# Both MLPs of a two-layer encoder by one level of Strassen's scheme: seven block products for eight

## The chip, the cores and the metric

The kernel runs on one core of one Trainium2 chip. The metric is the time of one execution on the device, in microseconds (us). The kernel before took 2733.05 us (median of three runs, 2729.04 to 2734.89). Every time below is of these runs or of one profiled execution of the same kernel. A core's engines run side by side and wait for one another through semaphores: PE (TensorE: matrix products, with its weight loads as PEld), DVE (VectorE), ACT (ScalarE), POOL (GpSimd) and SP (SyncE, which issues the transfers).

## What is computed

Two layers on a residual stream x of 1024 tokens by 1024 channels, float32. Layer 0 has differential attention beside an S5 state-space mixer, layer 1 a bidirectional HGRN2 recurrence. After each mixer stands an MLP, which is all that matters here:

```python
h = rmsnorm(x, norm_mlp_g[l])
x = x + jnp.square(jax.nn.relu(h @ w_ff_in[l])) @ w_ff_out[l]   # 1024 -> 4096 -> 1024
```

At the end comes one more RMSNorm.

## The kernel before

x stays in SBUF for the whole kernel as eight tiles `xT[d]`, 128 channels by 1024 tokens each. Every float32 product is made of three products of a reduced float format (fp32r): each operand is cut into a high part and the remainder, and wh·xh, wl·xh and wh·xl are summed in PSUM. `split` (L89 to L96) does the cutting: ACT casts the high part (L92, or L95 with a factor), and DVE or POOL subtracts it to get the low part (L93, or L96 with a factor). `load_w` (L98) brings a 512 KB weight tile (`raw`) and splits it. `mm_part` (L107 to L121) issues the matmuls, 512 columns each, with a weight load of its own for each.

An MLP (`mlp`, L192 to L235) takes `xg`, the split tiles of x times the norm's gain, which are made while the product before still runs (`new_xg`, called from the hooks `done`, `fin` and `last`). The factor R of each token, 1/rms, is applied behind the first product. The work goes by eight chunks of 512 hidden channels. Stage 1 of a chunk is four tiles of 48 matmuls: the product into PSUM (`big`), relu times R on DVE (L201), the square on POOL (L203), and a split. Stage 2 is eight tiles of 24 matmuls, each added to `xT[d]` by DVE from PSUM (L230). So the squares never leave SBUF, and each MLP has 3072 matmuls: 1536 in either product. In the last MLP the last chunk runs by token ranges (512, 256, 256), so that the final norm and the stores of one range lie beside the products of the next (L1207 is the final scaling).

The order of the instructions on each engine is fixed when the program is built: a scheduler places them by a simulated timeline (L1299), and each engine then runs its list in order. An instruction whose operand is late holds up everything behind it on its engine. Around the MLPs the code says: mixer 0, `out_even` (the attention's output projection and `new_xg`), `mlp`, mixer 1, `last_mlp`.

## Time and profile before

| | us |
|---|---|
| median of three runs | 2733.05 |
| the profiled execution, first to last instruction | 2730.3 |
| first MLP, about | 607 to 1310 |
| second MLP, about | 2031 to 2725 |
| PE busy over the span | 2627.0 (96%) |
| DVE busy | 1472.9 (54%) |
| ACT busy | 702.0 (26%) |
| POOL busy | 621.5 (23%) |

The profile describes one execution; its span is 2.75 us under the median of the runs, and inside their scatter. Busy shares are averages over stages with different limits: DVE's 54% is made of some 80 to 90% in the S5 part and a third in the MLPs. A timeline row gives the start, the duration and, in brackets, how long the engine had been idle and which engine's instruction ended that. Of two instructions in a row on one engine the second may start a little before the first's end, so the pace of an engine is read from start to start.

### The profile page before, as it was taken

To read this page: it belongs to the slowest core of one execution; us is meant where nothing else is said; L and a number is where in the kernel's file an instruction comes from. 1 tells how busy PE (TensorE), PEld (TensorE's weight loads), DVE (VectorE), ACT (ScalarE), POOL (GpSimd) and SP (SyncE) were. 2 spreads that over 40 slices of the span, in tenths; PEclk is the share of its full clock that TensorE was granted. 3 is DMA by queue.
4 is the path that set the end of the run, shared out by engine and by line. 5 is a ranking of instruction groups with operands and counts; after the bars stand their busy time and mean duration, and the time that the engine had idled before them with its cause. 6 is when DMAs were issued, how large, how long until landed. Compare 5 with 4: busy or idle time off the path is not lost.

```text
span 2730.3 us, 30693 instructions
## 1 busy us (share of the span) xinstructions
PE 2627.0 (96%) x12784; PEld 2201.2 (81%) x12784; DVE 1472.9 (54%) x1827; ACT 702.0 (26%) x1084; POOL 621.5 (23%) x403
## 2 busy tenths in 40 slices
PE   6878889999999999999999999999999999999997
PEld 5766778888888888888888888888888888888886
DVE  8788967665333233333576766666673333333336
ACT  3333356653111111111321222222241111111114
POOL 5555421111011101110122222222221111011102
PEclk9898999999999999999999999999999999999999
DMA  3222272301111111111111111111111111111112
GB/s 144 59 77 78 86 218 63 93 16 48 47 47 47 53 48 47 47 51 51 48 39 39 39 39 39 39 39 39 33 45 47 47 49 52 47 47 47 54 47 70
DMA packets 50554, 154.51 MB, mean 57 GB/s; under 512 B 7024, under 2 KB 13808, under 8 KB 50416
## 3 DMA queue, kind: packets, MB, share of 16 engines
q1 hardware_dynamic: 50416, 152.56, 17.7%
q8 instruction: 101, 1.65, 0.3%
q14 instruction: 37, 0.30, 0.0%
HBM read 131.56 MB, written 14.68 MB: 54 GB/s over the span
## 4 chain that ended last, share of the span: by engine, by line
PE 84%; DVE 10%; DMA 2%; issue 1%; ACT 1%; SPq 1%; POOL 1%; POOLq 0%; DVEq 0%; ACTq 0%
PE big L117 71%; PE sm L686 2%; PE big L1051 1%; PE sm L117 1%; PE sm L1007 1%; PE big L1022 1%; PE big L651 1%; PE big L652 1%; DVE z L514 1%; PE sm L676 1%; DVE z L517 1%; PE big L586 1%; DVE wl L93 1%; DMA raw<-w 1%; DMA kk<-dk 0%
## 5 line engine op out<-in xcount | busy, mean ns | idle before, releaser
L117 PE MATMUL big<-hi,wh 128*128 128x512 f32 x2000 | 627.0, 394 | 9.4 <-ACT hi L95 7.7
L117 PE MATMUL big<-lo,wh 128*128 128x512 f32 x2000 | 624.0, 393 | 10.9 <-DVE lo L96 10.9
L117 PE MATMUL big<-hi,wl 128*128 128x512 f32 x2000 | 623.0, 392 | 0.0
L92 ACT CAST wh<-raw 128x1024 fp32r<-128x1024 f32 x200 | 210.2, 1051 | 1375.0 <-PE big L117 1224.7
L117 PEld LDWEIGHTS big<-lo,wh 128*128 128x128 f32 x2000 | 376.5, 189 | 92.5 <-DVE lo L96 13.8
L117 PEld LDWEIGHTS big<-hi,wh 128*128 128x128 f32 x2000 | 374.9, 189 | 87.2 <-ACT hi L95 7.7
L117 PEld LDWEIGHTS big<-hi,wl 128*128 128x128 f32 x2000 | 377.3, 189 | 79.3 <-issue 0.2
L203 POOL TENSOR_TENSOR a<-a 128x1024 f32<-128x1024 f32 x64 | 172.8, 2701 | 1111.6 <-DVE a L201 1110.4
L230 DVE TENSOR_TENSOR x<-x,big 128x1024 f32<-128x1024 f32 x120 | 146.3, 1220 | 365.9 <-PE big L117 365.9
L117 PE MATMUL big<-ah,wl 128*128 128x512 f32 (+1 forms) x1008 | 314.6, 390 | 1.2 <-DVE wl L93 1.2
L117 PE MATMUL big<-ah,wh 128*128 128x512 f32 (+1 forms) x1008 | 313.5, 388 | 1.6 <-DVE x L220 1.6
L117 PE MATMUL big<-al,wh 128*128 128x512 f32 (+1 forms) x1008 | 311.5, 387 | 0.0
L201 DVE SCALAR_TENSOR_TENSOR a<-big,R 128x1024 f32<-128x1024 f32 x64 | 78.2, 1224 | 326.3 <-PE big L117 315.7
L117 PEld LDWEIGHTS big<-al,wh 128*128 128x128 f32 x1008 | 189.2, 188 | 41.9
L117 PEld LDWEIGHTS big<-ah,wl 128*128 128x128 f32 x1008 | 189.4, 188 | 41.5 <-DVE wl L93 1.6
L117 PEld LDWEIGHTS big<-ah,wh 128*128 128x128 f32 x1008 | 189.4, 188 | 41.1 <-DVE x L220 2.5
L93 POOL TENSOR_TENSOR wl<-raw,wh 128x1024 fp32r<-128x1024 f32 x58 | 139.4, 2403 | 333.5 <-ACT wh L92 325.0
L93 DVE TENSOR_TENSOR wl<-raw,wh 128x1024 fp32r<-128x1024 f32 x142 | 176.2, 1241 | 14.6 <-ACT wh L92 14.6
L93 DVE TENSOR_TENSOR al<-a,ah 128x1024 fp32r<-128x1024 f32 x64 | 80.7, 1260 | 169.2 <-ACT ah L92 169.1
L92 ACT CAST ah<-a 128x1024 fp32r<-128x1024 f32 x64 | 67.1, 1049 | 187.9 <-POOL a L203 187.9
L653 DVE TENSOR_REDUCE low<-big 128x1 f32<-128x1024 f32 x64 | 77.3, 1220 | 19.4 <-PE big L652 19.1
L655 ACT ACTIVATE E<-big,low 128x1024 f32<-128x1024 f32 x64 | 71.9, 1124 | 30.0 <-DVE low L653 30.0
(345 smaller groups left out, 3021.3 us busy)
## 6 DMA issues: line engine op xcount, KB each, us to landing
raw<-w SPq DMA_DIRECT2D x202, 512.0 KB, 3.3
x<-x SPq DMA_DIRECT2D x16, 512.0 KB, 8.2
sw<-qraw SPq DMA_DIRECT2D x32, 128.0 KB, 2.3
qa<-dq SPq DMA_DIRECT2D x16, 256.0 KB, 6.0
qb<-dq SPq DMA_DIRECT2D x16, 256.0 KB, 7.0
kk<-dk SPq DMA_DIRECT2D x16, 256.0 KB, 7.6
toep<-KK SPq DMA_DIRECT2D x64, 32.0 KB, 2.0
dq<-qh SPq DMA_DIRECT2D x4, 512.0 KB, 2.6
```

Source lines behind the costliest of these rows:

```text
L92: nc.scalar.copy(hi, src)
L93: (eng or nc.vector).tensor_tensor(lo, src, hi, ALU.subtract)
L117: nc.tensor.matmul(ps[:, t], a[:, s], b[:, t], start=(first and i == 0 and j == 0), stop=(last and i == n - 1 and j == 2),)
L201: nc.vector.scalar_tensor_tensor(a, ps, 0.0, R, ALU.max, ALU.mult)
L203: nc.gpsimd.tensor_tensor(sq, a, a, ALU.mult)
L230: nc.vector.tensor_tensor(xT[d], xT[d], ps, ALU.add)
L514: v.tensor_tensor_scan(fl(y, f)[:, 1:], fl(dec, f)[:, 0:last], fl(z, f)[:, 0:last], 0.0, ALU.mult, ALU.add)
L517: v.tensor_tensor_scan(fl(y, r)[:, 0:last][:, ::-1], fl(dec, r)[:, 1:][:, ::-1], fl(z, r)[:, 1:][:, ::-1], 0.0, ALU.mult, ALU.add,)
L586: self.nc.tensor.transpose(ps[:, 128 * j : 128 * j + 128], src[:, col0(j)], self.ident)
L653: v.tensor_reduce(low[:, c : c + 1], S, axis=AX.X, op=ALU.min)
L655: nc.scalar.activation(e, S, AF.Exp, bias=low[:, c : c + 1], scale=-1.0, accum_out=lsum[:, c : c + 1])
L686: nc.tensor.matmul(po, wT[:, k, :], A["V"][:, k, :], start=(k == 0), stop=(k == NT - 1))
```

## The change

Both products of both MLPs go by one level of Strassen's scheme in Winograd's form. The weights are cut in 2 by 2 blocks (`r11` to `r22`), and so are the activations (channels in two halves, tokens in two halves of 512). Seven block products then stand for eight, and each operand of a product is a block or a sum of blocks, formed on the chip in float32 and split afterwards.

- `combos` makes the seven right sides of two 128-channel tiles from four 512-column blocks: four POOL instructions (L253) and seven splits (`h` by ACT, `l` by DVE, L103). `left_sides` does the same for the weights: four loads, four POOL instructions (L316 to L324), seven splits.
- `seven` issues the seven products (in the order 1, 6, 5, 7, 2, 3, 4) into three PSUM banks a, b, c, of which there are two sets. ACT copies product 1 away (L349); DVE forms `v` and `w` from bank b less product 1 (L351, L353), since bank b goes on accumulating. Each product has 12 matmuls in a full step.
- `stage1`: 16 steps of 84 matmuls give 256 hidden channels each. DVE subtracts and applies relu times R, ACT squares, and the squares go to DRAM, 1 MB a step.
- `stage2` reads the squares back (`second_rows`), forms their right sides and adds the products to x: four DVE and three POOL instructions a step (L402 to L411). A step takes 512 hidden channels, half of them new: the right sides lie in four slots, of which the new pair takes two. The first and the last step take one pair alone, with 6 matmuls a product.
- `entry` makes the right sides of the first product from x, behind the mixer's last addition; `tail` does the last 512 hidden channels of the last MLP plainly (192 matmuls), with the final norm by token ranges as before.
- x is loaded earlier (`load_xT` ahead of the attention), and buffers are cut anew. HGRN2's operands are made after the first MLP's end.

An MLP's first product then has 16 × 84 = 1344 matmuls. The second has 14 steps of 84 and 4 of 42 in the first MLP, 1344; in the last MLP 12 of 84, 4 of 42 and the tail's 192, so 1368.

```diff
+    def combos(self, slots, rows):
+        gp = self.nc.gpsimd
+        Ts = [{} for _ in slots]
+        def put(p, srcs):
+            for T, slot, src in zip(Ts, slots, srcs):
+                pool = self.t01 if slot < 2 else self.t23
+                T[p] = tuple(self.half(f"{n}{slot % 2}{p}", pool=pool, dt=F32R) for n in "hl")
+                self.split(*T[p], src)
+        def each(op, outs, lefts, rights):
+            for o, x, y in zip(outs, lefts, rights):
+                gp.tensor_tensor(o, x, y, op)
+        b11, b12, b21, b22 = ([r[:, k] for r in rows] for k in range(4))
+        t2 = [self.half("t2", 2) for _ in slots]
+        put(1, b11)
+        each(ALU.subtract, b11, b11, b12)
+        each(ALU.add, t2, b22, b11)
+        put(6, t2)
+        put(5, b11)
+        each(ALU.subtract, b12, b12, b22)
+        put(7, b12)
+        put(2, b21)
+        put(3, b22)
+        each(ALU.subtract, t2, b21, t2)
+        put(4, t2)
+        return Ts
+    def entry(self, xT, gbase):
+        nc = self.nc
+        Ts = []
+        for i in range(4):
+            y = self.pe.tile([P, 4, 512], F32, tag="ar", name="y", bufs=2)
+            for j in range(2):
+                d = i + 4 * j
+                nc.scalar.activation(
+                    y[:, 2 * j : 2 * j + 2], xT[d].rearrange("p (h t) -> p h t", h=2), AF.Copy, scale=self.gcol(gbase, d)
+                )
+            Ts += self.combos((i if gbase == 16 else (i + 2) % 4,), [y])
+        self.square_sum(xT, PAIRED, "a0", "a1")
+        return Ts
...
+    def left_sides(self, src, n):
+        nc = self.nc
+        gp = nc.gpsimd
+        c = 128 * n
+        r = {}
+        for k, (tag, bufs) in enumerate((("r11", 2), ("r12", 1), ("r21", 2), ("r22", 2))):
+            r[tag] = self.half(tag, bufs, self.pv)[:, 0:c]
+            nc.sync.dma_start(r[tag], src[k])
+        def put(x):
+            hi, lo = (self.half(t, 7, self.pv, F32R)[:, 0:c] for t in ("wh", "wl"))
+            self.split(hi, lo, x)
+            return hi, lo
+        s1, s2 = (self.half(t, 1, self.pv)[:, 0:c] for t in ("s1", "s2"))
+        gp.tensor_tensor(s1, r["r21"], r["r22"], ALU.add)
+        gp.tensor_tensor(s2, s1, r["r11"], ALU.add)
+        yield put(r["r11"])
+        yield put(s2)
+        yield put(s1)
+        gp.tensor_tensor(r["r21"], r["r21"], r["r11"], ALU.add)
+        yield put(r["r21"])
+        yield put(r["r12"])
+        gp.tensor_tensor(s2, s2, r["r12"], ALU.add)
+        yield put(s2)
+        yield put(r["r22"])
+    def seven(self, src, Ts, take):
+        nc = self.nc
+        n = len(Ts)
+        left = self.left_sides(src, n)
+        a, b, c = (self.ps_f.tile([P, 512], F32, tag=t, name=t) for t in "abc")
+        bank = {1: a, 2: a, 6: b, 7: b, 4: b, 5: c, 3: c}
+        p1, vv, ww = self.half("p1"), self.half("v"), self.half("w")
+        v = nc.vector
+        for p in PRODUCTS:
+            hi, lo = next(left)
+            for i in range(n):
+                s = slice(128 * i, 128 * i + 128)
+                th, tl = Ts[i][p]
+                for j, (x, y) in enumerate(((hi, th), (lo, th), (hi, tl))):
+                    nc.tensor.matmul(
+                        bank[p], x[:, s], y,
+                        start=(p in (1, 6, 5) and i == 0 and j == 0), stop=(i == n - 1 and j == 2),
+                        skip_group_check=True,
+                    )
...
+    def stage1(self, l, Ts, spill):
+        nc = self.nc
+        v = nc.vector
+        R = [self.R[:, 0:512], self.R[:, 512:1024]]
+        for j in range(FF // 256):
+            out = self.pe.tile([P, 4, 512], F32, tag="ar", name="sq")
+            def put(k, src):
+                t = self.half("ct", 3)
+                if k != 0:
+                    v.tensor_tensor(t, *src, ALU.subtract)
+                    src = (t,)
+                v.scalar_tensor_tensor(t, src[0], 0.0, R[k % 2], ALU.max, ALU.mult)
+                nc.scalar.activation(out[:, k], t, AF.Square)
+            def take(p, a, b, c, p1, vv, ww):
+                if p == 7:
+                    put(3, (ww, c))
+                elif p == 2:
+                    put(0, (a,))
+                elif p == 3:
+                    put(1, (c, vv))
+                elif p == 4:
+                    put(2, (b, p1))
+            self.seven(self.io[f"win{l}"][j], Ts, take)
+            nc.sync.dma_start(spill[j], out.rearrange("p k t -> p (k t)"))
+    def second_rows(self, k, l, spill):
+        rows = []
+        for j in (2 * k, 2 * k + 1):
+            y = self.pe.tile([P, 4, 512], F32, tag="ar", name="y", bufs=2)
+            self.nc.sync.dma_start(y.rearrange("p k t -> p (k t)"), spill[j])
+            rows.append(y)
+        return self.combos((0, 1) if k % 2 != l else (2, 3), rows)
+    def stage2(self, src, Ts, qs, xT, fin=None):
+        v, gp = self.nc.vector, self.nc.gpsimd
+        for n, q in enumerate(qs):
+            (x11, x12), (x21, x22) = ((xT[d][:, 0:512], xT[d][:, 512:1024]) for d in (q, q + 4))
+            def take(p, a, b, c, p1, vv, ww):
+                if p == 7:
+                    v.tensor_tensor(x22, x22, c, ALU.subtract)
+                    gp.tensor_tensor(x22, x22, ww, ALU.add)
+                elif p == 2:
+                    v.tensor_tensor(x11, x11, a, ALU.add)
+                elif p == 3:
+                    v.tensor_tensor(x12, x12, c, ALU.add)
+                    gp.tensor_tensor(x12, x12, vv, ALU.subtract)
+                elif p == 4:
+                    v.tensor_tensor(x21, x21, b, ALU.add)
+                    gp.tensor_tensor(x21, x21, p1, ALU.subtract)
+            self.seven(src[n], Ts, take)
+            if fin:
+                fin(q)
+    def mlp(self, l, xT, Ts, fin=None):
+        spill = [self.pd.tile([P, 2048], F32, tag=f"sq{j}", name=f"sq{j}") for j in range(FF // 256)]
+        self.open_sums()
+        self.stage1(l, Ts, spill)
+        self.open_sums()
+        four, two = self.io[f"wout{l}"], self.io[f"wtwo{l}"]
+        rows = lambda k: self.second_rows(k, l, spill)
+        now = rows(0)
+        self.stage2(two[0], now, (2, 3), xT)
+        for k in range(1, 8 - l):
+            new = rows(k)
+            self.stage2(four[k - 1], now + new, (0, 1) if k % 2 else (2, 3), xT, fin if k == 7 else None)
+            now = new
+        self.stage2(two[1], now, (2, 3) if l == 0 else (0, 1), xT, fin)
...
+    def tail(self, xT, spill):
+        nc, io = self.nc, self.io
+        v = nc.vector
+        self.close_fast(2)
+        with self.pool("tl") as pt:
+            acts = []
+            for j in (14, 15):
+                y = self.pe.tile([P, 2, SEQ], F32, tag="ar", name="y", bufs=2)
+                nc.sync.dma_start(y.rearrange("p f t -> p (f t)"), spill[j])
+                for f in range(2):
+                    n = len(acts)
+                    acts.append(tuple(pt.tile([P, SEQ], F32R, tag=f"{t}{n}", name=t) for t in ("ah", "al")))
+                    self.split(*acts[-1], y[:, f])
+            ws = {}
...
+        xT = load_xT()
...
-            xT = load_xT()
...
     mix, xT = T.mixer0(load_xT)
-    xg = out_even(mix, xT)
-    xg = mlp(W_FF0, xT, xg, 8)
-    xg = T.mixer1(xg, xT)
-    last_mlp(W_FF1, xT, xg)
+    for _ in T.out_proj(0, mix, PAIRED, xT):
+        pass
+    T.st_b.close()
+    T.st_w.close()
+    T.st_m.close()
+    T.open_fast()
+    Ts = T.entry(xT, 16)
+    acc = []
+    def fin(q):
+        if q == 0:
+            acc.extend(T.half("t2", 2) for _ in range(2))
+        for d in (q, q + 4):
+            T.square_add(acc, xT[d], d == 0, True)
+    T.mlp(0, xT, Ts, fin)
+    T.finish_rstd(T.pc, acc)
+    T.close_fast(0)
+    T.open_hgrn()
+    xg = [None] * ND
+    for d in PAIRED:
+        xg[d] = T.new_xg(d, xT[d], T.gcol(8, d))
+    T.psum(3, 0, 2)
+    T.mixer1(xg, xT)
+    T.st_w.close()
+    T.st_a.close()
+    T.open_fast()
+    Ts = T.entry(xT, 24)
+    spill = T.mlp(1, xT, Ts)
+    T.tail(xT, spill)
```

The order of DVE at the end of the attention's output projection, before (x7, x0, x1, x2 are tiles of x; `lo` is the low part of xg, `acc` the sum of squares):

```order
L868 TENSOR_TENSOR x7_2951<-x7_2951,big_5237 128x1024
L96 SCALAR_TENSOR_TENSOR lo7_5264<-x7_2951,vec_72,hi7_5263 128x1024
L179 TENSOR_TENSOR acc_5127<-acc_5127,sq_5267 128x1024
L868 TENSOR_TENSOR x0_2937<-x0_2937,big_5276 128x1024
L179 TENSOR_TENSOR acc_5127<-acc_5127,sq_5302 128x1024
L868 TENSOR_TENSOR x1_2939<-x1_2939,big_5305 128x1024
L93 TENSOR_TENSOR wl_5452<-raw_5449,wh_5451 128x1024
L179 TENSOR_TENSOR acc_5127<-acc_5127,sq_5331 128x1024
L868 TENSOR_TENSOR x2_2941<-x2_2941,big_5340 128x1024
L96 SCALAR_TENSOR_TENSOR lo0_5396<-x0_2937,vec_72,hi0_5395 128x1024
```

And in the changed kernel, from the last two additions to x on (`l01` is the low part of right side 1 in slot 0, `wl` that of a left side, `a0` and `a1` the sums of squares):

```order
L1131 TENSOR_TENSOR x3_2760<-x3_2760,big_5311 128x1024
L1131 TENSOR_TENSOR x7_2768<-x7_2768,big_5337 128x1024
L298 TENSOR_TENSOR a0_5530<-a0_5530,sq_5534 128x512
L103 TENSOR_TENSOR l01_5391<-y_5386,h01_5390 128x512
L103 TENSOR_TENSOR wl_5643<-r11_5630,wh_5642 128x512
L103 TENSOR_TENSOR l02_5410<-y_5386,h02_5409 128x512
L103 TENSOR_TENSOR l03_5414<-y_5386,h03_5413 128x512
L103 TENSOR_TENSOR l11_5427<-y_5422,h11_5426 128x512
L103 TENSOR_TENSOR l12_5446<-y_5422,h12_5445 128x512
L103 TENSOR_TENSOR l13_5450<-y_5422,h13_5449 128x512
L298 TENSOR_TENSOR a1_5531<-a1_5531,sq_5537 128x512
L103 TENSOR_TENSOR wl_5660<-s2_5639,wh_5659 128x512
```

Before, the low parts of xg stand between the additions to x, so each is made as its tile is finished. Now all of the right sides stand behind the last addition, x7.

DVE in the middle of the second product of the first MLP, before:

```order
L230 TENSOR_TENSOR x0_2937<-x0_2937,big_6254 128x1024
L230 TENSOR_TENSOR x1_2939<-x1_2939,big_6280 128x1024
L93 TENSOR_TENSOR wl_6367<-raw_6364,wh_6366 128x1024
L230 TENSOR_TENSOR x2_2941<-x2_2941,big_6312 128x1024
L230 TENSOR_TENSOR x3_2943<-x3_2943,big_6338 128x1024
L93 TENSOR_TENSOR wl_6425<-raw_6422,wh_6424 128x1024
L230 TENSOR_TENSOR x4_2945<-x4_2945,big_6370 128x1024
L230 TENSOR_TENSOR x5_2947<-x5_2947,big_6396 128x1024
L93 TENSOR_TENSOR wl_6483<-raw_6480,wh_6482 128x1024
```

And in the changed kernel, in a full step of the second product (`l02`, `l07` right sides of slot 0, `l12`, `l17` of slot 1, a, b, c the banks in PSUM):

```order
L410 TENSOR_TENSOR x4_2762<-x4_2762,b_9108 128x512
L103 TENSOR_TENSOR wl_9550<-r12_9469,wh_9549 128x512
L402 TENSOR_TENSOR x6_2766<-x6_2766,c_9463 128x512
L351 TENSOR_TENSOR v_9253<-b_9250,p1_9252 128x512
L103 TENSOR_TENSOR wl_9568<-s2_9476,wh_9567 128x512
L103 TENSOR_TENSOR wl_9586<-r22_9473,wh_9585 128x512
L103 TENSOR_TENSOR l02_9436<-y_9391,h02_9435 128x512
L103 TENSOR_TENSOR l12_9440<-y_9393,h12_9439 128x512
L405 TENSOR_TENSOR x1_2756<-x1_2756,a_9249 128x512
L103 TENSOR_TENSOR wl_9622<-r11_9609,wh_9621 128x512
L103 TENSOR_TENSOR l07_9428<-y_9391,h07_9427 128x512
```

Before, one subtraction from SBUF (`wl`) stands between two additions from PSUM. Now two or three subtractions with both sources in SBUF stand between the instructions that read a bank.

POOL in the first MLP, before (in both products it has only the squares):

```order
L203 TENSOR_TENSOR a2_5758<-a_5756 128x1024
L203 TENSOR_TENSOR a2_6053<-a_6051 128x1024
L203 TENSOR_TENSOR a2_6116<-a_6114 128x1024
L203 TENSOR_TENSOR a2_6179<-a_6177 128x1024
L203 TENSOR_TENSOR a2_6242<-a_6240 128x1024
```

And in the changed kernel, in the second product (`t2` and `y` are sums of blocks of the squares, `s2` one of the weights):

```order
L253 TENSOR_TENSOR y_9037<-y_9037 128x512
L253 TENSOR_TENSOR t2_9041<-y_9037 128x512
L253 TENSOR_TENSOR y_9037<-y_9037 128x512
L253 TENSOR_TENSOR y_9039<-y_9039 128x512
L411 TENSOR_TENSOR x5_2764<-x5_2764,p1_8544 128x512
L253 TENSOR_TENSOR t2_9042<-y_9039 128x512
L253 TENSOR_TENSOR y_9039<-y_9039 128x512
L317 TENSOR_TENSOR s2_9122<-s1_9121,r11_9113 128x512
L253 TENSOR_TENSOR t2_9041<-y_9037,t2_9041 128x512
L408 TENSOR_TENSOR x2_2758<-x2_2758,v_8757 128x512
L253 TENSOR_TENSOR t2_9042<-y_9039,t2_9042 128x512
L324 TENSOR_TENSOR s2_9122<-s2_9122,r12_9115 128x512
```

POOL's squares are gone (ACT makes them), and in their place stand the sums of blocks and a part of the additions to x.

## Rows read from the trace of the kernel before

**Rows 1.** The page: span, and busy time, share and instructions of each engine.
```profile
span 2730.3 us, 30693 instructions
...
PE 2627.0 (96%) x12784; PEld 2201.2 (81%) x12784; DVE 1472.9 (54%) x1827; ACT 702.0 (26%) x1084; POOL 621.5 (23%) x403
```

**Rows 2.** The page's chain of work that ended last, its shares by engine.
```profile
PE 84%; DVE 10%; DMA 2%; issue 1%; ACT 1%; SPq 1%; POOL 1%; POOLq 0%; DVEq 0%; ACTq 0%
```

**Rows 3.** Windows inside the MLPs (busy us and instructions by engine, PEclk, DMA share, GB/s).
```profile
1250.00:1300.00 50.00, 50.00 (x222) 41.22 (x221) 14.32 (x12) 6.31 (x6) 5.19 (x2) 1.00 0.15 52
1300.00:1350.00 50.00, 50.00 (x220) 41.04 (x219) 34.52 (x28) 22.92 (x22) 7.57 (x3) 1.00 0.14 45
2000.00:2050.00 50.00, 48.25 (x228) 39.89 (x227) 33.45 (x25) 23.09 (x24) 18.25 (x8) 1.00 0.13 43
2600.00:2650.00 50.00, 50.00 (x221) 41.14 (x220) 15.37 (x13) 5.26 (x5) 2.74 (x1) 1.00 0.16 53
```

**Rows 4.** Timeline of ACT in the first MLP (start us, us, engine, line).
```profile
699.02 1.05 ACT L92 CAST wh<-raw 128x1024 fp32r<-128x1024 f32 x1 [5.69 <-PE big L117]
...
732.00 1.05 ACT L92 CAST wh<-raw 128x1024 fp32r<-128x1024 f32 x1 [9.94 <-PE big L117]
```

**Rows 5.** Groups by line and shape (busy us, mean ns of one | idle before).
```profile
L117 PE MATMUL big<-hi,wh 128*128 128x512 f32 x2000 | 627.0, 394 | 9.4 <-ACT hi L95 7.7 <-DVE x L1086 1.6 <-DVE a L201 0.2
...
L92 ACT CAST wh<-raw 128x1024 fp32r<-128x1024 f32 x200 | 210.2, 1051 | 1375.0 <-PE big L117 1224.7 <-issue 83.3 <-POOL rn L1058 61.4
...
L93 DVE TENSOR_TENSOR wl<-raw,wh 128x1024 fp32r<-128x1024 f32 x142 | 176.2, 1241 | 14.6 <-ACT wh L92 14.6
L203 POOL TENSOR_TENSOR a<-a 128x1024 f32<-128x1024 f32 x64 | 172.8, 2701 | 1111.6 <-DVE a L201 1110.4 <-DVE al L93 1.2
...
L93 POOL TENSOR_TENSOR wl<-raw,wh 128x1024 fp32r<-128x1024 f32 x58 | 139.4, 2403 | 333.5 <-ACT wh L92 325.0 <-issue 8.5
...
L96 DVE SCALAR_TENSOR_TENSOR lo<-x,vec,hi 128x1024 fp32r<-128x1024 f32 x28 | 43.3, 1554 | 10.8 <-ACT hi L95 10.6
```

**Rows 6.** Timeline of DVE in the S5 part, two-source instructions.
```profile
163.50 1.53 DVE L288 TENSOR_TENSOR gtr<-gtr,tm 128x512 f32<-128x512 f32 x1
164.96 1.76 DVE L525 TENSOR_TENSOR z<-z,wr 128x512 f32<-128x512 f32 x1
166.65 1.76 DVE L526 TENSOR_TENSOR z<-z,wi 128x512 f32<-128x512 f32 x1
```

**Rows 7.** Timeline of POOL in the same stretch.
```profile
163.16 1.32 POOL L426 TENSOR_TENSOR dec<-edge,sp 128x512 f32<-128x512 f32 x1
164.45 1.72 POOL L291 TENSOR_TENSOR gti<-gti,tm 128x512 f32<-128x512 f32 x1
166.13 1.73 POOL L448 TENSOR_TENSOR tm<-hq,cc 128x640 f32<-128x640 f32 x1
167.82 1.72 POOL L451 TENSOR_TENSOR tm<-hq,cc 128x640 f32<-128x640 f32 x1
```

**Rows 8.** Lines L503 and L504, DVE with one source in PSUM (ns min/median/max).
```profile
L503 DVE TENSOR_TENSOR z<-side,wr x8: 677/687/692, 120.0 to 336.4; 128x512 f32<-128x512 f32 x8
...
L504 DVE TENSOR_TENSOR z<-side,wi x8: 674/680/681, 120.6 to 337.0; 128x512 f32<-128x512 f32 x8
```

**Rows 9.** Timeline of DVE near the end: 256 columns, and a tiny instruction.
```profile
2709.45 0.42 DVE L179 TENSOR_TENSOR acc<-acc,sq 128x256 f32<-128x256 f32 x1 [0.42 <-ACT sq L178]
2709.80 0.15 DVE L142 TENSOR_SCALAR rs_v<-sm 128x2 f32<-128x2 f32 x1
2709.87 0.41 DVE L220 TENSOR_TENSOR x<-x,big 128x256 f32<-128x256 f32 x1
```

**Rows 10.** The page's DMA issues (KB each, median us to landing).
```profile
raw<-w SPq DMA_DIRECT2D x202, 512.0 KB, 3.3
x<-x SPq DMA_DIRECT2D x16, 512.0 KB, 8.2
```

**Rows 11.** One window of the S5 part.
```profile
200.00:250.00 50.00, 39.21 (x197) 33.41 (x198) 41.42 (x48) 19.72 (x40) 26.69 (x21) 0.83 0.26 85
```

More of the change, by code (lines that the diff above doesn't have):

```diff
@@ new lines, in open_fast @@
+    def open_fast(self):
+        self.st_f = [ExitStack() for _ in range(3)]
+        self.pv, self.t01, self.t23 = (
+            st.enter_context(self.pool(n, side="right")) for st, n in zip(self.st_f, ("pv", "t01", "t23"))
+        )
+        self.st_e = None
+        self.open_sums()
+        if self.ps_stack:
+            self.ps_stack.close()
+        self.ps_stack = ExitStack()
+        self.ps_f, self.ps_sm = (
+            self.ps_stack.enter_context(self.tc.tile_pool(name=n, bufs=2, space=PSUM, reuse_waits="tile"))
+            for n in ("psx", "pss")
+        )
@@ new lines, in open_sums, with close_fast, half @@
+    def open_sums(self):
+        if self.st_e:
+            self.st_e.close()
+        self.st_e = ExitStack()
+        self.pe = self.st_e.enter_context(self.pool("pe"))
+    def close_fast(self, n):
+        if n == 0:
+            self.st_e.close()
+        while len(self.st_f) > n:
+            self.st_f.pop().close()
+    def half(self, tag, bufs=1, pool=None, dt=F32):
+        return (pool or self.pe).tile([P, 512], dt, tag=tag, name=tag, bufs=bufs)
+    def combos(self, slots, rows):
[23 more added lines that the diff above has]
+        return Ts
@@ new lines, in square_sum, with square_add @@
+    def square_sum(self, xT, order, *tags):
+        accs = [self.half(t) for t in tags]
+        for n, d in enumerate(order):
+            self.square_add(accs, xT[d], n == 0)
+        self.finish_rstd(self.pc, accs)
+    def square_add(self, accs, x, first, wide=False):
+        nc = self.nc
+        tmp = self.pe.tile([P, 4, 512], F32, tag="ar", name="sq", bufs=2) if wide and not first else None
+        for h, acc in enumerate(accs):
+            sq = acc if first else self.half("sq") if tmp is None else tmp[:, h]
+            nc.scalar.activation(sq, x[:, 512 * h : 512 * h + 512], AF.Square)
+            if not first:
+                nc.vector.tensor_tensor(acc, acc, sq, ALU.add)
@@ new lines, in seven @@
+    def seven(self, src, Ts, take):
[16 more added lines that the diff above has]
+                        skip_group_check=True,
+                    )
+            if p == 1:
+                nc.scalar.copy(p1, a)
+            elif p == 6:
+                v.tensor_tensor(vv, b, p1, ALU.subtract)
+            elif p == 7:
+                v.tensor_tensor(ww, b, p1, ALU.subtract)
+            take(p, a, b, c, p1, vv, ww)
@@ L699, in attn_store @@
         if half == 0:
-            mix[h] = tuple(self.pg.tile([P, SEQ], F32R, tag=f"{n}{h}", name=f"{n}{h}") for n in ("hi", "lo"))
+            mix[h] = tuple(self.pm.tile([P, SEQ], F32R, tag=f"{n}{h}", name=f"{n}{h}") for n in ("hi", "lo"))
         ps = self.small()
@@ L817, in mixer0 @@
         s5ctx.close()
+        xT = load_xT()
+        self.st_m = ExitStack()
+        self.pm = self.st_m.enter_context(self.pool("pm", side="right"))
         mix = [None] * ND
@@ L857, in glu, with out_proj @@
             yield
-    def out_proj(self, part, mix, order, xT, done=None, w=None):
+    def out_proj(self, part, mix, order, xT, w=None):
         xs = mix[4 * part : 4 * part + 4]
@@ L1076, in hgrn_mix, with hgrn_out @@
         yield
-    def hgrn_out(self, hs, os, xT, last=None):
+    def hgrn_out(self, hs, os, xT, order=range(ND)):
         n = len(hs)
-        for d in range(ND):
-            if d % (ND // n) == 0:
+        for d in order:
+            if n == 2 and d % 4 == 0 or d == 0:
                 w = self.load_w(W_OUT_O + hs[0] + d * n // ND, self.nc.gpsimd)
@@ L1142, in mixer1 @@
             run(proj, 9)
-            run(self.hgrn_out((7,), [H["o"]], xT, last), 9)
-            self.finish_rstd(pc, acc[0])
-        return out
+            run(self.hgrn_out((7,), [H["o"]], xT, PAIRED), 9)
 @with_exitstack
```

227 lines of the change are left out of this document (94 added, 133 removed).

## The prediction

> **What bounds the kernel now.** I read the page's busy line first: PE 2627.0 of 2730.3 us, DVE 54%, POOL 23% [rows 1]. The chain of waits says the same, 84% of it on PE [rows 2]. But a share is a mean over stages, so the windows come next. Inside the MLPs PE is busy 50.00 of 50 us at full clock (PEclk 1.00), DVE for 14 to 15 us and POOL for 3 to 5 [rows 3]. Between 1300 and 1350, where the first MLP ends and its output is split for the next mixer, PE is still at 50.00. Only the entry of the second MLP loses something: 48.25 [rows 3]. There are as many weight loads as matmuls [rows 1], so a matmul with its own weights is what the pace below already contains.
>
> The MLPs are thus bound by the number of matmuls alone. The pace is read from the casts of the weight tiles, one for every 48 matmuls: 699.02 to 732.00 is three tiles, 32.98 / 144 = 0.229 us a matmul [rows 4].
>
> **The gain.** Two times 3072 matmuls become 1344 + 1344 and 1344 + 1368 (12 × 84 + 4 × 42 + 192): 744 fewer, 744 × 0.229 = -170.4 us. This holds as far as the other engines keep up; the rest of the sum is where they don't.
>
> **What the added work costs.** A DVE instruction of 512 columns with a PSUM source goes at one per 0.60 us (L503 starts at 120.0, L504 at 120.6) and takes 672 to 692 ns in S5, where POOL is busy over half of the time [rows 8, 11]: POOL doesn't slow it. With both sources in SBUF it is otherwise. In S5 DVE takes 1.76 us for 512 columns at 164.96 and 166.65 [rows 6], while POOL's take 1.72 and start at 164.45, 166.13 and 167.82; the one just before, without such company, took 1.32 [rows 7]. So the two take turns: a pair, one of each, goes per 1.685 us, of which 0.60 is DVE's and 1.085 POOL's. Almost all that the change adds on DVE (splits, L103) and on POOL (L253, L316 to L324, the additions to x) is of this kind. The splits of before took 1241 ns at 1024 columns [rows 5], nearly undisturbed, but there POOL had one square per tile of 11 us.
>
> The Trainium skill, "SBUF — State Buffer", section "Who interferes with whom", states this as a rule: a DVE instruction with two SBUF inputs contends with a GpSimd instruction that reads SBUF, and the shared port is an exclusive lock. The trace agrees that they wait for each other, not that they exclude each other for their whole length, which would be 0.60 + 1.32 = 1.92 a pair and not 1.685. By the full lock the sum below would be some 88 us higher (374 pairs, 174 and 152 in the second products and 24 at each entry, by 0.235).
>
> **Stage 1.** Each of the 16 steps has 84 × 0.229 = 19.2 us of PE. DVE has 7 splits, two instructions for v and w, three subtractions and four relus, 16 in all; POOL 4. With the port: 4 × 1.685 + 12 × 0.60 = 13.9 us. ACT has 7 casts, a copy and 4 squares, each about half of a 1024-wide cast's 1.05 [rows 5], some 7 us. A step moves 1 MB in and 1 MB out in 19 us, about 105 GB/s, against 85 in a window of S5 [rows 11] and 53 here [rows 3]. PE stays the bound: cost nothing. What hides it is PE's 19.2; 5 us of slack is left on DVE.
>
> **Stage 2.** Here the right sides come on top. A full step of two output pairs has 168 × 0.229 = 38.5 us of PE. DVE has 28 splits and 12 PSUM instructions (24 us alone), POOL 22 (8 for left sides, 8 for right, 6 additions; 22 × 1.32 = 29 us alone): each alone would be hidden. By the port they need 22 × 1.685 + 6 × 0.60 = 40.7, already over PE's 38.5, if all 12 PSUM instructions fit into POOL's turns. Over the first MLP: 174 POOL and 222 DVE two-source instructions of 512 columns, and a few narrow ones at 0.35 [rows 9]: 174 × 1.685 + 48 × 0.60 + 14 = 336 us, against 1344 × 0.229 = 308 of PE. If none of the 108 PSUM instructions fits, 65 more: 401. They stand in DVE's order between splits and wait for PE's banks, and right sides may be written only as a slot is freed; so not all fits. I take a third of them in the way: 358, +50. In the second MLP likewise 152 × 1.685 + 30 × 0.60 + 16 = 290, PE 1176 × 0.229 = 269, 96 PSUM instructions: up to 348, taken 309, +40. Ends for both together: 0 (PE hides all, if the contention of S5 doesn't repeat here) and +172.
>
> **Entries.** Before, xg is made between the last additions to x, and nothing waits for R but 1.75 us of PE [rows 3]. Now all right sides stand on DVE behind the addition of x7, and PE can do only the first products of two steps (72 matmuls, 16.5 us) until `v` is made. Up to `v` DVE has 55 two-source instructions and POOL 24: 24 × 1.685 + 31 × 0.60 = 59 us, and about 1.5 until x7 and the first weights (3.3 us to landing [rows 10]) are there. PE idles 59 + 1.5 - 16.5 = 44. At the second MLP DVE has 51: 56.6 - 16.5 - 1.75 = 38. Ends: each 25 without contention, when ACT is next (41 casts and 16 squares at half of 1.05, 8 at 1.05, some 40 us), and 50.
>
> **Exit of the first MLP.** PE was busy 50.00 there [rows 3]. Now x7's last addition, some 45 tiny DVE instructions at 0.07 to 0.15 [rows 9] and the first splits (1.55 each [rows 5]) stand ahead of PE, which needs a split per 6 matmuls (1.4 us): +9, between 5 and 15.
>
> **Small terms.** Each stage 1 to stage 2: the squares must go to DRAM and back (512 KB land in 3.3 us when alone, in 8.2 when 16 are queued [rows 10]) and be split, while PE has products left: +4 each, +8, between 0 and 20. After a long idle the clock may start low; in the worst window of S5 it was 0.83 [rows 11]: a few us per entry, under DVE's work, +4 in all. x's 4 MB go earlier on SP, ahead of S5's last loads: +2, between 0 and 10. POOL's squares vanish, under PE before: 0.
>
> **Sum.** -170.4 + 50 + 40 + 44 + 38 + 9 + 8 + 4 + 2 = +24.6. The profiled span of 2730.3 is inside the scatter of the runs, so the difference goes on the median: 2733 + 25 = 2758 us. About 0.2% (5.5 us) is what can be told from no change.
>
> **Rivals.**
> - The port doesn't set the pace of stage 2: DVE and POOL run far enough ahead that their turns fall under PE. For it: the low mean of L93 on DVE beside L203 on POOL [rows 5]. Against it: the port needs 40.7 of 38.5 us. Without the +90 it is 2733 - 170.4 + 105 = 2668, faster; half of it gives 2713. It decides from the point where the excess in stage 2 is under 60 us.
> - The PSUM instructions hold up DVE so that no turn overlaps: stage 2 at 401 and 348, +172 for +90: 2840.
> - The short gaps in stage 2 bring the clock down, as in S5, where PE is busy 39.21 of 50 us and the clock is 0.83 [rows 11]. At 0.83 the 308 us become 371 and the 269 become 324, 13 and 15 above my stage 2: 2786. In the MLPs now nothing of it is seen (1.00 [rows 3]).
> - The scheduler's order lets the first products start so early that the entries cost 20 each, not 41: 2716. Against it: the rows of the order behind x7.
>
> The Trainium skill, "TensorE: Matmul & The Clock Gate", section "A second HAM failure mode: psum-queue depth-cycling", describes the third rival: micro-idles between groups of matmuls that cycle through banks make the clock oscillate. S5's windows are in keeping with it; that stage 2 does it no run here shows.
>
> **Chances.** Forecast (2715 to 2800) 0.47, stage 2 hidden (2650 to 2715) 0.22, no overlap (2800 to 2850) 0.18, clock 0.08, cheap entries 0.05. The small part of the forecast's case below 2727.5 (0.03), the second and the last give faster 0.30; within 0.2% 0.08; slower 0.62. For 8 in 10 I leave out half of the hidden case's lower part and the upper end of the case without overlap: 2690 to 2825; the forecast's own range is 2715 to 2800.
>
> **What would show it.** Right: in stage 2 DVE's L103 of 512 columns at 1.2 to 1.8 us and L253 near 1.7, PE in windows of stage 2 at 42 to 46 of 50, waiting for `l` and `wl` of DVE; an idle of some 40 us at each entry; 19.2 to 19.5 us per step of stage 1. Wrong: stage 2 at 38.5 us a step, or entries with PE busy; or, the other way, stage 1 slower than 19.5 a step, which would mean that the 0.229 doesn't hold for these products.

## The result: 2843 us, 4% slower, and the profile after

The changed kernel took 2843.12 us (median of four runs, 2840.2 to 2845.39), the kernel before 2733.64 beside it: ratio 1.0405, interval 1.039 to 1.042. The forecast was 2758 us. It had the direction, and less than a quarter of the size: +25 forecast, +110 measured. The time lies by the rival in which no turn overlaps, 2840 us; the experiments below show that this rival's reason was not the right one either.

The page after (span, busy time, the chain's shares), to be read beside [rows 1, 2]:

```profile
span 2843.0 us, 32513 instructions
...
PE 2542.8 (89%) x12040; PEld 2093.0 (74%) x12040; DVE 2084.8 (73%) x2692; ACT 1040.9 (37%) x1846; POOL 1237.6 (44%) x853
...
PE 62%; DVE 21%; issue 6%; POOL 5%; DMA 3%; ACT 2%; SPq 1%; POOLq 0%; DVEq 0%; ACTq 0%
```

PE has 744 fewer matmuls (12784 to 12040) and works 84 us less, in a span that is 113 us longer. DVE went from 1473 to 2085 us, POOL from 622 to 1238, and of the chain PE keeps 62% where it had 84%.

Windows of the changed kernel, columns as in [rows 3]: the first entry, the start of stage 1 behind it, the place between the first MLP's two products, the middle of its second product, and stage 1 of the second MLP:

```profile
650.00:700.00 50.00, 25.14 (x54) 14.62 (x54) 47.48 (x46) 28.05 (x49) 35.21 (x22) 0.52 0.09 27
700.00:750.00 50.00, 46.74 (x215) 38.89 (x214) 31.27 (x41) 18.77 (x32) 16.02 (x11) 0.97 0.22 74
1000.00:1050.00 50.00, 27.87 (x92) 20.06 (x91) 36.40 (x42) 20.75 (x40) 26.38 (x18) 0.73 0.38 139
1150.00:1200.00 50.00, 44.64 (x182) 36.00 (x181) 41.12 (x44) 18.72 (x32) 36.31 (x24) 0.93 0.28 90
...
2200.00:2250.00 50.00, 50.00 (x222) 41.43 (x221) 29.50 (x41) 18.39 (x31) 13.36 (x10) 1.00 0.37 121
```

Stage 1 is as it was forecast: PE 50.00 of 50. In the second product PE works 44.64 of 50, DVE 41 and POOL 36. At the entry PE's 25 us are at half the clock (0.52), and the place between the products has 28 us.

The stages, by the first and last matmul of each (a full step of the second product has 38.5 us of PE). The MLPs of the kernel before run from about 642 to 1344.8 us and from 2003.7 to 2715.6 by the matmuls of its trace, not to 1310 and from 2031 as the table ahead of the prediction has it:

| | forecast over the matmuls' own time | measured |
|---|---|---|
| matmuls saved | -170 | -170 |
| first entry with stage 1 | +44 | 361.0 - 307.8 = +53 |
| first second product | +50 | 389.5 - 307.8 = +82 |
| second entry with stage 1 | +38 | 357.7 - 307.8 - 1.8 = +48 |
| second second product, with the tail | +40 | 375.7 - 313.3 - 8.2 = +54 |
| between the products, two places | +8 | 13.0 + 12.9 = +26 |
| exit of the first MLP | +9 | 673.1 - 657.3 = +16 |
| clock, earlier loads of x | +6 | +1.5, and the clock is in the rows above |
| sum | +25 | +110 |

Of each stage its matmuls at 0.229 us are taken off. The 1.8 us at the second entry and the 8.2 of the last product are what the second MLP of the kernel before took over its own 3072 matmuls. The exit goes from the last matmul of the MLP to the last one of the mixer behind it.

The groups of the changed kernel that the terms rest on (columns as in [rows 5]):

```profile
L103 DVE TENSOR_TENSOR wl<-r,wh 128x512 fp32r<-128x512 f32 x240 | 245.8, 1027 | 40.9 <-ACT wh L102 40.9
L103 DVE TENSOR_TENSOR l<-y,h 128x512 fp32r<-128x512 f32 x190 | 233.4, 1255 | 28.2 <-ACT h L102 25.0 <-PE b L343 1.5 <-PE a L343 0.9
...
L253 POOL TENSOR_TENSOR y<-y 128x512 f32<-128x512 f32 x76 | 128.5, 1694 | 73.9 <-DVE l L103 73.9
...
L351 DVE TENSOR_TENSOR v<-b,p 128x512 f32<-128x512 f32 x66 | 45.0, 681 | 14.7 <-ACT p L349 14.7
```

The contention is there, as in [rows 6, 7]: a subtraction of 512 columns takes 1.03 to 1.26 us on DVE in the mean where it takes 0.68 with POOL silent (the run with all sums on DVE, below), and POOL's sums take 1.69 where one took 1.32 [rows 7]. `v`, from PSUM, takes 0.68, as in [rows 8]. So the question is why a step took 46.5 us and not 43.

### The profile page after: what moved, and what is told of

The parts are those of the page before. It is cut to its first block, busy times and chain, and to the rows that moved or that the text cites. A ratio compares the mean times of both kernels' runs of the same rounds, so it can differ in the third digit from the quotient of the medians.

```text
span 2843.0 us, 32513 instructions
## 1 busy us (share of the span) xinstructions
PE 2542.8 (89%) x12040; PEld 2093.0 (74%) x12040; DVE 2084.8 (73%) x2692; ACT 1040.9 (37%) x1846; POOL 1237.6 (44%) x853
## 4 chain that ended last, share of the span: by engine, by line
PE 62%; DVE 21%; issue 6%; POOL 5%; DMA 3%; ACT 2%; SPq 1%; POOLq 0%; DVEq 0%; ACTq 0%
PE big L127 18%; PE b L343 13%; PE a L343 9%; PE c L343 8%; DVE l L103 5%; DVE wl L103 3%; PE sm L945 2%; PE big L1313 1%; PE sm L127 1%; POOL y L253 1%; PE tail L478 1%; PE sm L1269 1%; PE big L1284 1%; PE big L910 1%; DMA y<-sq 1%
## 5 line engine op out<-in xcount | busy, mean ns | idle before, releaser
L343 PE MATMUL b<-h,wh 128*128 128x512 f32 x744 | 299.6, 403 | 34.3 <-DVE w L353 15.0
L127 PE MATMUL big<-hi,wh 128*128 128x512 f32 x976 | 311.4, 399 | 12.8 <-ACT hi L105 11.4
L127 PE MATMUL big<-lo,wh 128*128 128x512 f32 x976 | 308.9, 396 | 13.9 <-DVE lo L106 13.9
L127 PE MATMUL big<-hi,wl 128*128 128x512 f32 x976 | 308.4, 396 | 0.0
L343 PE MATMUL b<-l,wh 128*128 128x512 f32 x744 | 296.0, 398 | 9.5 <-DVE l L103 9.5
L103 DVE TENSOR_TENSOR wl<-r,wh 128x512 fp32r<-128x512 f32 (+1 forms) x272 | 266.1, 982 | 46.6 <-ACT wh L102 46.6
L343 PE MATMUL b<-h,wl 128*128 128x512 f32 x744 | 296.3, 398 | 3.1 <-DVE wl L103 3.1
L103 POOL TENSOR_TENSOR wl<-raw,wh 128x1024 fp32r<-128x1024 f32 x58 | 144.2, 2487 | 326.2 <-ACT wh L102 317.3
L343 PE MATMUL a<-h,wh 128*128 128x512 f32 x496 | 205.0, 413 | 60.3 <-ACT h L102 28.8
L103 DVE TENSOR_TENSOR l<-y,h 128x512 fp32r<-128x512 f32 x190 | 233.4, 1255 | 28.2 <-ACT h L102 25.0
L343 PE MATMUL a<-h,wl 128*128 128x512 f32 x496 | 204.4, 412 | 13.5 <-DVE wl L103 13.5
L103 DVE TENSOR_TENSOR wl<-s,wh 128x512 fp32r<-128x512 f32 (+1 forms) x198 | 165.5, 836 | 49.4 <-ACT wh L102 48.3
```

The costliest lines, as they stand in the source:

```text
L103: (eng or nc.vector).tensor_tensor(lo, src, hi, ALU.subtract)
L127: nc.tensor.matmul(ps[:, t], a[:, s], b[:, t], start=(first and i == 0 and j == 0), stop=(last and i == n - 1 and j == 2),)
L343: nc.tensor.matmul(bank[p], x[:, s], y, start=(p in (1, 6, 5) and i == 0 and j == 0), stop=(i == n - 1 and j == 2), skip_group_check=True,)
```

## Experiments

Three theories stood at the start. Turns: DVE and POOL wait for each other, and this sets the pace. Chain: reading back, sums, casts and splits stand in series behind the freeing of the slots, whoever shares a port. Clock: the spells of half clock make the excess. A step is the time from one addition of L410 to the next but one, in the middle of the second product. Where no interval is given, the time is one run, beside 2730.27 us (the run of one mirror image below: 2730.24) of the kernel before on the same chip.

### DVE's second source from PSUM

```diff
-        (eng or nc.vector).tensor_tensor(lo, src, hi, ALU.subtract)
+        self.nc.vector.tensor_tensor(lo, src, self.kps[:, 0 : src.shape[1]], ALU.subtract)   # a bank of zeros
```

> The changed kernel, with one thing left out: the low parts of the MLPs' operands are formed from a constant bank in PSUM instead of the high part (the low parts are then wrong), so that each of these DVE instructions has one source in SBUF; counts, lengths and buffers stay. Theory 1, turns: DVE and POOL take turns at 1.69 us a pair, and this sets the pace of the second products (46.5 and 44.2 us a full step against 38.5 of PE) and of the entries (67 us to the first v). Then the DVE instructions fall to 0.60 each and POOL's to 1.32, a full step comes to 38.5 to 40 us, the entry to about 45, and the time to some 2680. Theory 2, chain: reading the squares back, sums, casts and splits of a step stand in series behind the slots' release, whoever shares a port; the shorter sums then give 2 us a step and the time stays over 2790. Theory 3, clock: the half-clock spells (3.4 us each, about one per 40 us) make the excess; the step stays above 43 as long as any gaps remain.

2765.92 us. About one full step of the second product, and the groups (columns as before):

```profile
1181.00:1219.00 38.00, 37.91 (x167) 31.08 (x167) 24.45 (x40) 17.49 (x30) 27.40 (x23) 1.00 0.30 100
```

```profile
L228 DVE TENSOR_TENSOR wl<-r,kps 128x512 fp32r<-128x512 f32 x232 | 155.1, 678 | 92.0 <-PE b L350 69.0 <-PE a L350 14.0 <-PE c L350 8.9
...
L228 DVE TENSOR_TENSOR l<-y,kps 128x512 fp32r<-128x512 f32 x190 | 119.7, 679 | 27.7 <-DMA y<-sq 22.5 <-PE b L350 5.0
...
L260 POOL TENSOR_TENSOR y<-y 128x512 f32<-128x512 f32 x76 | 99.7, 1321 | 108.5 <-DVE l L228 103.2 <-ACT h L227 5.0
```

DVE's subtractions fall to 0.68 us, POOL's sums to 1.32, PE is full at clock 1.00 and a step takes 38.5 us from the third full one on: in the steps the turns were the whole excess, and the clock's spells (27 us of half clock in 340 of the changed kernel) were a result of the gaps, not a cause. The chain theory, with a time over 2790, falls. The edit does change one thing more than its expectation says: a low part no longer waits for its high part's cast on ACT, so the series has lost a link (and the small sums in PSUM have one buffer where they had two). The run with all sums on DVE, below, keeps that link and also comes to 39.8 us a step; what both runs lack is the contention. But 2680 was missed by 86 us. The first steps still took 40 to 46, the places between the products 12.7 each, and the entries with stage 1 355.6 and 353.0, only 5 less each. There something else binds. Entry rows of this kernel, DVE from x7's addition to the first `v`, and ACT:

```profile
640.11 1.22 DVE L1138 TENSOR_TENSOR x<-x,big 128x1024 f32<-128x1024 f32 x1 [4.38 <-PE big L127]
...
695.28 0.68 DVE L358 TENSOR_TENSOR v<-b,p 128x512 f32<-128x512 f32 x1
```

```profile
671.43 0.63 ACT L303 ACTIVATE sq<-x 128x512 f32<-128x512 f32 x1 [1.17 <-DVE a L305]
...
681.41 0.63 ACT L303 ACTIVATE sq<-x 128x512 f32<-128x512 f32 x1 [3.05 <-DVE a L305]
```

It still takes 55 us to `v` (67 in the changed kernel, below). ACT's squares wait for DVE's additions to the norm's sum (L305), since there is one buffer for a square, and the additions have both sources in SBUF.

### The weights' sums on DVE, and its mirror image

```diff
     def left_sides(self, src, n):
-        gp = nc.gpsimd
+        gp = nc.vector
```

> The changed kernel with the weights' four sums of each step (L316 to L324) on DVE instead of POOL. By turns a full step has 14 x 1.085 + 36 x 0.60 = 36.8 us on the port (from 40.7), under PE's 38.5, so steps of 41 to 43 us and about 2790 to 2800. Chain: no change of the series, 2835 to 2845. If neither port nor chain but DVE's own order binds, it becomes slower, as DVE gets 8 instructions more a step: 2850 to 2870.

```diff
     def combos(self, slots, rows):
-        gp = self.nc.gpsimd
+        gp = self.nc.vector
```

> The changed kernel with the sums of the right sides (L253, 8 a step) on DVE, and the weights' sums (8 a step) left on POOL: the mirror image of the run with the weights' sums on DVE. The bare count of turns is the same for both, 14 x 1.085 + 36 x 0.60 = 36.8 us a full step, so if the count decides, both give steps of about 45.5 us and some 2835 us. If it decides where in the step POOL's instructions stand (the right sides' sums come in one burst of 8 when the slots are freed, each at 1.7 us and followed by casts and splits for which PE waits, while the weights' sums are made products ahead), this run has steps of 40 to 42 us and some 2770; the entry, where 16 of 24 POOL instructions are such sums, falls by 5 to 8 us.

The weights' sums on DVE: 2838.70 us, steps of 45 to 48; by turns 2790 to 2800 were expected, and the time alone would fit the chain theory (2835 to 2845), which the run before it rules out. The right sides' sums on DVE: 2793.22, steps of 42 to 43.5, entries with stage 1 355.2 and 351.9 (6 less each). That lies between the two expectations, 2835 by the count and 2770 by the place, nearer to the second. Both move 8 of 22 POOL instructions a step, and the count of turns is the same. A full step of each, in turn:

```profile
1141.00:1186.00 45.00, 40.37 (x169) 32.45 (x168) 42.63 (x48) 17.85 (x30) 22.69 (x14) 0.96 0.28 94
```

```profile
1174.00:1217.00 43.00, 40.03 (x168) 31.97 (x167) 37.57 (x48) 17.45 (x30) 21.19 (x15) 0.96 0.30 94
```

So the count over a whole step, on which the forecast's stage 2 rested, is refuted as a measure. DVE of the first, in one step:

```profile
1143.70 0.69 DVE L402 TENSOR_TENSOR x<-x,c 128x512 f32<-128x512 f32 x1 [1.14 <-PE c L343]
...
1152.16 0.69 DVE L353 TENSOR_TENSOR w<-b,p 128x512 f32<-128x512 f32 x1 [0.31 <-PE b L343]
...
1162.46 1.75 DVE L103 TENSOR_TENSOR l<-y,h 128x512 fp32r<-128x512 f32 x1
...
1166.03 1.76 DVE L103 TENSOR_TENSOR l<-y,h 128x512 fp32r<-128x512 f32 x1
```

Until about 1157 PE sets the pace: DVE has short waits for its banks, and POOL runs three instructions in 16 us. Then the slots are free, the right sides' 8 sums come on POOL, and the splits beside them take 1.75 us each. The shared port is little used in one half of the step and sets the pace in the other. The two runs differ in more than the place, though: with the right sides' sums on DVE, their splits wait no longer for a sum of POOL. How much of the 3 to 4 us a step that makes was not tried.

### All sums and additions on DVE

```diff
     # combos, left_sides and stage2
-        gp = self.nc.gpsimd
+        gp = self.nc.vector
```

> The changed kernel with all sums and additions of the MLPs on DVE, POOL idle there. By turns nothing contends any more: a full step has 62 x 0.60 = 37.2 us of DVE against 38.5 of PE, steps of 39.5 to 42, an entry 79 x 0.60 = 47 us to v instead of 67, and about 2740 to 2765. Chain: steps stay at 44 to 46, about 2820. If DVE's in-order list (now 97% full in a step) binds, steps of 43 to 45 and about 2800.

2749.34 us, 94 less than the changed kernel, with 518 instructions more on DVE (2692 to 3210). Two full steps, and groups:

```profile
1160.00:1200.00 40.00, 38.81 (x170) 31.57 (x169) 38.31 (x64) 17.83 (x31) 0.00 (x0) 1.00 0.32 107
1200.00:1240.00 40.00, 38.81 (x170) 31.51 (x170) 38.31 (x63) 17.68 (x30) 0.00 (x0) 1.00 0.31 108
```

```profile
L103 DVE TENSOR_TENSOR wl<-r,wh 128x512 fp32r<-128x512 f32 x240 | 163.8, 684 | 33.0 <-ACT wh L102 32.8
...
L103 DVE TENSOR_TENSOR l<-y,h 128x512 fp32r<-128x512 f32 x190 | 127.1, 685 | 32.8 <-ACT h L102 23.3 <-PE b L343 9.2
...
L253 DVE TENSOR_TENSOR y<-y 128x512 f32<-128x512 f32 x76 | 51.9, 682 | 0.0
```

Steps of 39.8 us, as expected by turns: with POOL silent a two-source instruction of 512 columns takes 0.68 us (0.60 from start to start), and 62 of them fit under PE with 1.3 us lost. The entries with stage 1 fell by 9 and 13 us, to 351.7 and 344.7.

### One pool of buffers for both products

```diff
         self.stage1(l, Ts, spill)
-        self.open_sums()
...
-            out = self.pe.tile([P, 4, 512], F32, tag="ar", name="sq")
+            out = self.pe.tile([P, 4, 512], F32, tag="ar", name="sq", bufs=2)
...
-                t = self.half("ct", 3)
+                t = self.half("ct", 2)     # and the sums t2 with the same tag
```

> The changed kernel without the new cut of the buffers between the first and the second product (one pool for both, two buffers for the squares, two for the sums). The 13 us in which PE stands at that place in each MLP are put down to the first two reads of squares, which wait until the last store has freed their buffer. One of the two now goes ahead of the last store: if that is the cause, 3 to 5 us less at each place, some 2835; if the reads wait for the stores' data or for the slots, 13 us stay and the time does not change.

2811.65 us, 31 less. In the changed kernel, around the first of the two places (start us, us, engine, line):

```profile
1004.42 0.39 PE L343 MATMUL c<-l,wh 128*128 128x512 f32 x1
...
1008.36 0.33 SPq L383 DMA_DIRECT2D sq<-sq  x1
1012.28 0.80 SPq L390 DMA_DIRECT2D y<-sq  x2
1017.18 1.66 ACT L102 CAST h<-y 128x512 fp32r<-128x512 f32 x3 [8.85 <-DMA y<-sq]
...
1017.86 0.80 PE L343 MATMUL a<-h,wh 128*128 128x512 f32 x1 [13.05 <-ACT h L102]
```

The last store is issued at 1008.36, the two reads at 1012.28 when it has landed, and the first cast starts at 1017.18: the last squares, their store and the reads stand in series, 13.05 us of PE. With one pool:

```profile
995.82 0.38 SPq L390 DMA_DIRECT2D y<-sq  x1
...
1000.41 0.39 PE L343 MATMUL c<-l,wh 128*128 128x512 f32 x1
...
1001.15 1.66 ACT L102 CAST h<-y 128x512 fp32r<-128x512 f32 x3
...
1001.81 0.19 PEld L343 LDWEIGHTS a<-h,wh 128*128 128x128 f32 x1 [1.44 <-ACT h L102]
```

One read was issued before the last store, PE waits 1.0 us. 24 us go at the two places, where 3 to 5 each were expected: PE starts on the first read's right sides alone. Of the rest, 4 us lie ahead of the first entry, where nothing was changed (the attention's projection ends at 643.8 in the profile of the changed kernel and between 638 and 642 in the others); the first second product became 8 shorter, with steps of 44 us, and the last one 7 longer.

### Together, and the norm's sum on PE

> All sums and additions of the MLPs on DVE, and one pool of buffers for both products. If the two gains are of different places (93 us in steps and entries, 24 us of the two 13 us stops between the products, 7 more in steps), they add up but for those 7: 2718 to 2727, a little faster than the kernel before. If the freed stop only lets PE run into DVE's backlog earlier, less than 12 us of the 31 are left: over 2737.

2732.74 us, ratio 1.0003 (0.9994 to 1.0013): level with the kernel before, and between the two expectations. Of the 24 us, 17 were left: the places shrank to 1.4 and 1.0, but the products behind them take 347.7 and 356.5 (with the tail) where they took 345.8 and 352.4. Part of DVE's backlog had probably been worked off while PE stood; no run shows it by itself.

```diff
-            if not first:
-                nc.vector.tensor_tensor(acc, acc, sq, ALU.add)
+                for k in range(4):      # 128 columns each, into two banks
+                    nc.tensor.matmul(sums[h][:, c], sq[:, c], self.ones, start=(n == 0), stop=(n == ND - 1), ...)
```

> The same, and the sums of squares at the entries made by PE in PSUM (64 matmuls of 128 columns an entry with the matrix of ones) instead of 14 additions on DVE, with two buffers for the squares. If the entry is bound by DVE's list (47 us of two-source instructions) and by ACT's squares that wait for DVE, 14 x 0.60 = 8.4 us and some of the waits go at each entry: 2697 to 2710. If casts and splits of the right sides alone set it, or PE's small matmuls at the low clock take the time back (64 at 0.12 to 0.24 us), no change: 2715 to 2727.

2718.02 us, ratio 0.9956 (0.994 to 0.9972): 15 us under the run without PE's sums, where 17 and more were counted; the range expected was reckoned from 2718 to 2727 for that run, which took 2733. The output of this kernel is off by 0.11 in relative terms: a start mark stands at each of a bank's four regions, and parts of the first tile's squares seem to be missing from the norm's sum. The next kernel marks only the first region, and is otherwise the same:

> All sums and additions of the MLPs on DVE, one pool of buffers for both products, and the sums of squares at the entries made by PE, with the start of a bank's sum marked once a bank instead of once a region. The same instructions as in the run before it of this kind, so the same time: 2712 to 2726, about 0.4% under the kernel before. If that run's gain hung on a chance of its runs (2714 to 2725), 2730 as without PE's sums.

2718.94 us, ratio 0.9959 (0.9946 to 0.9972), as expected: the fastest version with a right output, 0.4% under the kernel before. The first entry with stage 1 fell from 351.7 to 338.6, the second only from 344.8 to 343.9; there `v` comes 3.7 us sooner, but PE has done 65 matmuls by then and not 74, and why was not tried.

```diff
     def stage2(self, src, Ts, qs, xT, fin=None):
-        v, gp = self.nc.vector, self.nc.vector
+        v, gp = self.nc.vector, self.nc.gpsimd
```

> The same, with the three additions to x of each step of the second product that have both sources in SBUF (L403, L408, L411) on POOL again: 6 a full step. DVE then has 44 two-source instructions and 12 from PSUM (33.6 us alone), POOL 6. If PSUM instructions fill POOL's turns, the step falls from 40.0 to PE's 38.5 and the time by some 10 to 15 us; if a turn of POOL simply costs DVE 1.085 us where its own instruction took 0.60 and nothing overlaps, 33.6 + 6.5 = 40.1 and no change; if these additions, each behind a bank's read, hold up the next product's buffers (v, w and product 1 have one buffer each), slower, steps of 42.

2726.46 us, ratio 0.9988 (0.9978 to 0.9997), slower than the one before it. Steps of 40.4 to 41.2 in the first MLP and 38.0 to 40.3 in the second, for 39.9: six turns of POOL a step cost as much as DVE's own six instructions, or a little more. That is nearest to the second of the three expectations, but the time was 7.5 us longer and not unchanged; the second product of the first MLP takes 356.1 us for 349.1.

## Why the prediction was wrong

**What was right.** The matmuls' pace and stage 1 (PE 50.00 of 50). That DVE and POOL take turns at 1.69 us a pair, read from two stretches of the S5 part, and that this undoes the gain: without POOL 94 of the 110 us go. That the entries and the exit cost what PE had done under other work before. Most of the signs named came as well (PE 44.64 of 50 in stage 2, L253 at 1.69 us), which shows how little they told the forecast from a step 3.5 us longer.

**The step that failed: stage 2, "I take a third of them in the way: 358".** It measured 389.5, near the end of 401 that I had left to a rival. With 14 us of the same kind in the second MLP that is 46 of the 85 us that the sum missed; the entries have 19, the places between the products 18, the exit 7, and the clock term was 5 too high. The error was in how the count was used. 22 turns and 40 DVE instructions were summed over a step and set against PE's 38.5, as if they could be spread over it; only the PSUM instructions were thought to stand in the way. But the right sides can be written only when a slot is free. DVE and POOL of the changed kernel, one full step (the bracket is the idle time before, and what ended it):

```profile
1146.49 0.87 DVE L103 TENSOR_TENSOR wl<-r,wh 128x512 fp32r<-128x512 f32 x1 [0.84 <-ACT wh L102]
1148.78 0.69 DVE L410 TENSOR_TENSOR x<-x,b 128x512 f32<-128x512 f32 x1 [1.42 <-PE b L343]
...
1151.28 0.69 DVE L402 TENSOR_TENSOR x<-x,c 128x512 f32<-128x512 f32 x1 [0.83 <-PE c L343]
...
1166.70 3.48 DVE L103 TENSOR_TENSOR l<-t,h 128x512 fp32r<-128x512 f32 x2
1170.11 1.75 DVE L103 TENSOR_TENSOR l<-y,h 128x512 fp32r<-128x512 f32 x1
1171.78 0.68 DVE L410 TENSOR_TENSOR x<-x,b 128x512 f32<-128x512 f32 x1
...
1173.46 1.77 DVE L103 TENSOR_TENSOR l<-y,h 128x512 fp32r<-128x512 f32 x1
```

```profile
1160.79 1.67 POOL L403 TENSOR_TENSOR x<-x,w 128x512 f32<-128x512 f32 x1 [4.84 <-DVE w L353]
...
1166.26 1.68 POOL L253 TENSOR_TENSOR y<-y 128x512 f32<-128x512 f32 x1 [0.62 <-DVE l L103]
1167.90 1.74 POOL L321 TENSOR_TENSOR r<-r,r 128x512 f32<-128x512 f32 x1
1169.60 1.71 POOL L253 TENSOR_TENSOR y<-y 128x512 f32<-128x512 f32 x1
1171.28 1.72 POOL L253 TENSOR_TENSOR t<-y 128x512 f32<-128x512 f32 x1
```

From 1146 to 1165 PE sets the pace: it never stops, DVE waits for it here and there (1.42 and 0.83 us ahead of L410 and L402), and POOL stands still for 4.84 us ahead of L403. From 1166.26 on POOL runs one sum behind the other at 1.69 us, and DVE's splits take 1.75. PE then stops, and not for a split itself: it waits for a bank that one of DVE's additions has to free, and the addition stands behind splits in DVE's list. The chain of waits at the first of the step's two stops, and PE's waits for the two additions from 1055 to 1395 us (in all, times, longest):

```profile
1168.41 3.45 DVE l L103 x2
1171.86 0.61 DVE x L410
...
1172.51 4.61 PE b L343 x12
```

```profile
PE a L343 <- DVE x L405: 15.4, 5, 3.2
...
PE b L343 <- DVE x L410: 12.6, 6, 3.4
```

From 1101 to 1335, five steps, PE stands for 6.1 us a step, and the half clock behind the stops (20 us in all) costs some 2 more: 38.5 + 6 + 2 = 46.5, not the 43 of my mean nor the 40.7 of the count. PE binds one part of the step and the port the other, and the two add up. The mirror-image runs fit this: the same count, and 3 to 4 us of difference a step. I had named the slots ("right sides may be written only as a slot is freed") and put no price on them. The rival with no overlap came close by luck. Its PSUM instructions take 0.67 to 0.69 us throughout, and where the port binds they do fit into POOL's turns: L410 and the split behind it take 1.68 us together (1171.78 to 1173.46). They cost by their place behind the splits.

The Trainium skill, "SBUF — State Buffer", section "Who interferes with whom", also says that a DVE instruction with at most one SBUF input does not contend with GpSimd, outside the modes that use two ports. The run with the second source in PSUM agrees: 678 and 679 ns beside POOL's sums. That run also sets a sum of the prediction right. The 1.92 us a pair of a full lock added a pace (0.60) to a duration (1.32); POOL alone goes at 1.25 from start to start (1202.64, 1203.89, 1205.14), so it would be 1.85, still over the 1.69 measured.

**Between the products: 4 us each, measured 13.** I took 3.3 us for a load and left PE products for the rest. What I missed is that the buffers are cut anew there, so that the first read waits for the last store: 3.9 us to the store's issue, 3.9 for the store and 4.9 for the reads stand in series with nothing left for PE.

**Entries: 44 and 38, measured 53 and 48.** The changed kernel's DVE from x7's addition to the first `v`:

```profile
643.79 1.22 DVE L1131 TENSOR_TENSOR x<-x,big 128x1024 f32<-128x1024 f32 x1 [4.38 <-PE big L127]
...
710.76 0.68 DVE L351 TENSOR_TENSOR v<-b,p 128x512 f32<-128x512 f32 x1
```

That is 67.0 us; 60.5 were forecast. The turns were counted right in kind: without POOL 9 and 13 us went, 12 were counted. At the first entry the count left out that DVE itself waits, 8 us in all, most of it for ACT's squares and casts and for PE's sum of the squares. At the second it hardly waits (0.5 us), and `v` comes after 58.5 us where 56.6 were counted; there PE has done 56 matmuls by `v` and not the 72 that the sum took for granted, some 4 us. The rest, 3 to 4 us at each, is lost behind `v`. Taking the additions off DVE gave 13 us at the first entry and 1 at the second, so their share differs too.

**Clock.** Its rival (+28) did not come as such. The spells are there (a granted clock of 0.93 to 0.96 in the steps, at most 14 us in 340), and in the steps they go when the gaps go (1.00). Over the whole second product of the first MLP, with its start behind the 13 us stop, the clock is 0.93, which is 26 us of 389.5 at most; no run took the clock alone away.

**Still open.** The second entry, which gains 1 us from PE's sums; how much of the 3 to 4 us between the mirror images is the place alone; and the best version's entries, which still cost 31 and 36 us over the matmuls, and its second product's 39.9 us a step, 1.4 over PE.
